# The RWKV part of a decoder layer, from a planner's order to two interleaved streams in a fixed matrix-engine order

## The chip, the cores and the metric

The kernel runs on one core of a Trainium2 chip. The metric is the device time of one launch in microseconds (us), here 2481.27 us as the median of three runs (2479.97 to 2483.46). A core has a matrix engine (PE, with its weight loads PEld), a vector engine (DVE), a scalar engine (ACT), a general engine (POOL) and a queue that issues most DMAs (SP). Each engine runs its own instructions in order; instructions of different engines wait for each other through semaphores.

## The reference, cut to what matters

One decoder layer on 256 tokens with 2048 channels, all in float32. A product with `w_in` feeds three mixers (SSD, RWKV-7, mLSTM) and three gates; each mixer's output is projected, gated and added, then `w_out`, a norm, a convolutional feed-forward block and a norm follow. The change is about RWKV and the gates:

```
proj = h @ w_in
(..., rwkv_p, ..., gate_pre) = split(proj)
merged = (g_ssd * (y_ssd @ proj_ssd) + g_rwkv * (y_rwkv @ proj_rwkv) + g_mlstm * (y_mlstm @ proj_mlstm))

def rwkv7_mixer(p, ...):
    p = p + (token_shift(p) - p) * mu
    r, k, v, w_lo, a_lo, g_lo = split(p)
    decay = exp(-exp(-softplus(-(w0 + tanh(w_lo) @ w2)) - 0.5))
    a = sigmoid(a0 + a_lo @ a2);  g = sigmoid(g_lo) @ g2
    kk = heads(k * k_k);  kk = kk * rsqrt(max(sum(kk * kk), 1e-24))
    kh = heads(k * (1 + (a - 1) * k_a))
    # per step: S = S diag(w) + (S (-kk)) (kk a)^T + v kh^T ;  y = S r
    y = head_layer_norm(recurrence(r, decay, kh, v, -kk, kk * a)) * ln_w + ln_b
    return (y + sum(r * kh * r_k) * v) * g
```

## The kernel before, in words

Weights are float32 and are multiplied in three passes of a reduced float32 type: `chunks` loads two row tiles of 512 columns (512 KB, SP queue, four `wraw` buffers), ACT casts the high half `whi` (L163), and DVE subtracts to get the low half `wlo` (L164); three buffers of each. `proj_cm` then issues 12 products of 128x256 for each row tile (L176, L178, L180), `block_tm` six of 128x512 (L194 to L196, the "wide" ones of the gates). A *chunk* is two row tiles. The loop over chunks is issued at high priority; apart from that, the order of the instructions on every engine is a scheduler's, which simulates the program with a cost for each instruction and picks what is ready.

RWKV's recurrence is done in chunks of 64 tokens, for 4 groups of 8 heads (512 channels). `rwkv_group(g)` first has the products for r, k, v and the gate of branch 1, then the small steps: decays `cs` and `pext`, the norm of k (`nr`, its two halves `nrr`, spread to all rows by L523 and L524, giving `nk` at L525), POOL's `kh` and `av` (L532, L534), and the operands `l1e`/`l1o` (even and odd heads) and `bk`, half on POOL (L552, L554) and half on DVE. Their pair products (L560) go into `bp` with a mask (DVE, L562) and into the other half of l1 (ACT copy L564, POOL mask L565). The diagonal 32x32 blocks of bp are inverted by columns: four DVE transposes (`ni`, L595) bring the matrices into one layout, then 31 steps of two instructions (L610, L612) on the tiles `yi` and `si` run at the same time on DVE (5 columns of the result) and POOL (the other 27). Two transposes to `x1` (L619) and four to `xt` (L622) bring the result back; small products (L630, L639) combine two blocks into one of 64x64. Then four recurrence steps follow (L654 to L688, on `zm`, `zve`, `zvo`), the output gate (L703), and the tail with the head norm and `yo` (L709 to L732).

After the four groups come SSD (two blocks of B and C, then two blocks for each of four groups) and the branches 1, 0, mLSTM and 2. The planner is free to move SSD's weight products up between RWKV's small steps, and does: RWKV and SSD together end at about 897 us. Branch 1 reads its gates from memory (`gdram`), branches 0 and 2 make theirs in `branch` as they go.

`smalls` (its helper lines L403 to L443) prepares the decays of SSD and mLSTM once, by scans on DVE (`s_da`) and small products (L412, L414, L443).

Of the kernel before, what the change touches and what calls it, by code (L numbers as in the profile page):

```python
# [17 lines left out]
P = 128  # L18
# [16 lines left out]
C_R = 5152  # L35
# [20 lines left out]
CONSTS = [("ones", 1), ("head2", 32), ("maskg", 192), ("mneg", 128), ("scanm", 256)]  # L56
# [20 lines left out]
def const_array():  # L77
# [11 lines left out]
    c[:, COFF["scanm"]:COFF["scanm"] + 256] = (np.arange(256) % 64 != 0)[None]  # L89
    c[:, COFF["eps"]:COFF["eps"] + 4] = np.array([1e-5, 64e-5, 1e-6, 1.0], np.float32)[None]  # L90
# [3 lines left out]
class Pair:  # L94
# [8 lines left out]
    def l(self, kt):  # L103
        return self.lo[kt // self.n][:, kt % self.n]


class Layer:
# [61 lines left out]
    def proj_cm(self, W, pieces, cts, X, nkt=KT):  # L169
        nc = self.nc  # L170
        acc = [self.psA.tile([P, 2, T], F32, name="acc") for _ in range((len(cts) + 1) // 2)]
        for kt, wh, wl in self.chunks(W, nkt, pieces):
            for j, (o, m) in enumerate(cts):
# [7 lines left out]
                                 stop=kt == nkt - 1, skip_group_check=True)  # L181
        return [acc[j // 2][:m, j % 2] for j, (o, m) in enumerate(cts)], acc
# [4 lines left out]
    def block_tm(self, W, c0, X, nkt=KT, pages=()):  # L187

# [10 lines left out]
        for kt, wh, wl in self.chunks(W, nkt, [(0, c0, 512)], pages):  # L199
            mm(0, kt, wh, wl)  # L200
            if kt // KC < (nkt + KC - 1) // KC - len(pages):
                mm(1, kt, wh, wl)
            else:
                late.append((kt, wh, wl))
        for w in late:
            mm(1, *w)
# [248 lines left out]
    def rwkv_group(self, g):  # L455
        nc, tc, a = self.nc, self.tc, self.a
        W = a["w_in"]
        vec, gps = nc.vector, nc.gpsimd

        lw = self.lw if g else self.load_lora(0)  # L460

        rkv = []
        for i, (nm, c0, pi) in enumerate((("r", C_R, 0), ("k", C_K, 1), ("v", C_V, 2 + g % 2))):
            cts, _ = self.block_cm(W, c0 + g * 512, self.X)
            t = self.p4(pi, nm)
            for j in range(4):
                self.lerp(cts[j], t[:, j], self.v("mu_" + nm, 4 * g + j),
                          self.omm[:, 16 * i + 4 * g + j:16 * i + 4 * g + j + 1])
            rkv.append(t)
            if g == 0 and i == 0:  # L470
                self.smalls()
        if g == 0:
            for o, i_ in self.spill:
                nc.sync.dma_start(out=o, in_=i_)
        gate = self.gate(1, g, 18)
        nc.scalar.dma_start(out=self.gdram[:, g], in_=gate)
        r, k, v = rkv

# [27 lines left out]

        sq = self.p4(7, "sq")
        for j in range(4):
            nc.scalar.activation(out=sq[:, j], in_=k[:, j], func=AF.Square, scale=self.v("k_k", 4 * g + j))
        ps = self.bank()  # L510
# [7 lines left out]
        self.split(nrr[:, 0], nrr[:, 1], nr)  # L518
        nk = self.p4(8, "nk")
        for ct in range(4):  # L520
# [5 lines left out]
                                     in1=ps, op0=ALU.mult, op1=ALU.mult)  # L526

# [4 lines left out]
        gps.tensor_tensor(out=kh, in0=kh, in1=k, op=ALU.mult)  # L532

        gps.tensor_tensor(out=av, in0=av, in1=nk, op=ALU.mult)  # L534

        sq = self.p4(7, "sq")
        for j in range(4):
            vec.scalar_tensor_tensor(out=sq[:, j], in0=r[:, j], scalar=self.v("r_k", 4 * g + j),
                                     in1=kh[:, j], op0=ALU.mult, op1=ALU.mult)


        L1, BK, BP, ZV = self.L1, self.BK, self.BP, self.ZV
# [4 lines left out]
        PL = self.cp.tile([P, 16], F32, name="pl", bufs=2)  # L547
        vec.tensor_copy(out=PL, in_=pe[:, :, 64])
        for c in range(4):
            for e in range(2):  # L550
# [4 lines left out]
                vec.tensor_tensor(out=uc(BK)[h, c, :, o], in0=ch(kh)[h, c], in1=ch(cs)[h, c], op=ALU.mult)  # L555
            for e in range(2):
                ps = self.bank().rearrange("p (c t) -> p c t", c=4)
                for p in range(4):
                    u = 4 * p + c
                    nc.tensor.matmul(ps[:, p], lhsT=BK[H[e], u], rhs=L1[e][H[e], u], start=True, stop=True)  # L560
                mg = mge[e]
                vec.tensor_tensor(out=uc(BP)[H[e], c], in0=ps[H[e]], in1=mg[H[e]].to_broadcast([64, 4, P]), op=ALU.mult)  # L562
                lk = uc(L1[e])[H[1 - e], c]
                nc.scalar.copy(out=lk, in_=ps[H[1 - e]])  # L564
# [385 lines left out]
    def run(self, upto=None):  # L950
# [7 lines left out]
        for g in range(4):  # L958
            self.rwkv_group(g)
# [144 lines left out]
```

## Time and profile before

| | value |
|---|---|
| median of 3 runs | 2481.27 us |
| the profiled execution | 2480.85 us, of it 2479.1 us of span |
| PE busy in the span | 2397.7 us |
| DVE, ACT, POOL busy | 1681.8, 1250.0, 516.1 us |
| stretch of RWKV and SSD | about 90 to 897 us |
| PE busy in that stretch, granted clock | 762.31 of 807.00 us, 0.96 |
| DVE busy in that stretch | 688.10 us |

The profile's lines name an engine, an operation, the tile written and the tiles read, the shapes and a count; times are us, unless marked ns. The granted clock is the share of full speed that PE had. A line with `<-` behind a bracket names what ended the idle time ahead of the instruction. In a timeline, the first column is the start and the second the length; instructions of one kind that follow closely are merged with their count, and the next one can start before the length shown is over, since matrix products are pipelined. The span is the time between the first and last instruction; the launch's time is a little longer.

### The profile page before, as it was taken

The page shows a single profiled execution, that of the slowest core. Times are in us where ns is not written, and L with a number is a line of the kernel's source. Part 1 is how long each engine was busy: PE and PEld are TensorE (multiplying, and loading weights), DVE is VectorE, ACT ScalarE, POOL GpSimd, SP SyncE. Part 2 cuts the span into 40 slices and gives each one's busy share as a digit, 9 for nine tenths or more (in the row PEclk, how much of TensorE's full clock was granted, in tenths as well). Part 3 has the DMA queues.
Part 4 walks back from the last instruction along what each step waited for, and adds up shares of the span by engine and source line. Part 5 has one row for each costly group of instructions (what it writes and reads, how often), then busy time and mean ns, then how long its engine had stood idle before and what let it go on. Part 6 is the DMA issues. An engine that isn't in the chain of part 4 may idle for free.

```text
span 2479.1 us, 41687 instructions
## 1 busy us (share of the span) xinstructions
PE 2397.7 (97%) x16602; PEld 2164.2 (87%) x16602; DVE 1681.8 (68%) x2116; ACT 1250.0 (50%) x1634; POOL 516.1 (21%) x488
## 2 busy tenths in 40 slices
PE   7999998989999999999999999999999999999997
PEld 7988797887989988888988888887999999998886
DVE  6678988897997875545566665556765666665545
ACT  4555555454646654444456654444554454454333
POOL 0046463563643521001000021000300000000000
PEclk9999998998999999999999999999999999999999
DMA  8654435344445656666666666655655555557664
GB/s 239 187 162 126 134 103 151 86 137 141 121 140 163 193 182 213 211 195 192 184 186 178 181 211 213 188 192 190 186 182 186 181 182 185 186 167 229 195 196 148
DMA packets 280276, 435.09 MB, mean 176 GB/s; under 512 B 25432, under 2 KB 118032, under 8 KB 279696
## 3 DMA queue, kind: packets, MB, share of 16 engines
q1 hardware_dynamic: 278640, 427.70, 56.9%
q8 instruction: 130, 2.13, 0.4%
q10 hardware_dynamic: 864, 2.62, 0.3%
q0 software_dynamic: 576, 2.10, 0.2%
q14 instruction: 66, 0.54, 0.1%
HBM read 423.90 MB, written 8.43 MB: 174 GB/s over the span
## 4 chain that ended last, share of the span: by engine, by line
PE 83%; DVE 10%; issue 2%; POOL 2%; DMA 1%; ACT 1%; SPq 0%; DVEq 0%; POOLq 0%; ACTq 0%
PE acc L195 13%; PE acc L196 13%; PE acc L194 13%; PE acc L180 13%; PE acc L178 13%; PE acc L176 13%; DVE wlo L164 4%; PE mix L560 1%; DVE si L612 1%; DVE si L610 1%; DVE xt L622 1%; DMA wraw<-in_ffn_w_down 1%; DVE ni L595 1%; PE seq L685 1%; PE mix L797 0%
## 5 line engine op out<-in xcount | busy, mean ns | idle before, releaser
L164 DVE TENSOR_TENSOR wlo<-wraw,whi 128x1024 fp32r<-128x1024 f32 (+2 forms) x756 | 987.5, 1309 | 664.6 <-ACT whi L163 656.6
L163 ACT CAST whi<-wraw 128x1024 fp32r<-128x1024 f32 (+2 forms) x756 | 786.9, 1043 | 847.1 <-PE acc L196 427.6
L180 PE MATMUL acc<-xh,wlo 128*128 128x256 f32 x3104 | 889.3, 287 | 21.0 <-DVE wlo L164 20.8
L176 PE MATMUL acc<-xh,whi 128*128 128x256 f32 x3104 | 889.1, 287 | 3.3 <-ACT whi L163 3.1
L178 PE MATMUL acc<-xl,whi 128*128 128x256 f32 x3104 | 887.5, 286 | 0.0
L180 PEld LDWEIGHTS acc<-xh,wlo 128*128 128x128 f32 x3104 | 600.0, 194 | 29.5 <-DVE wlo L164 25.5
L176 PEld LDWEIGHTS acc<-xh,whi 128*128 128x128 f32 x3104 | 601.0, 194 | 9.1 <-ACT whi L163 3.5
L178 PEld LDWEIGHTS acc<-xl,whi 128*128 128x128 f32 x3104 | 601.0, 194 | 3.2 <-issue 1.0
L195 PE MATMUL acc<-wlo,xh 128*128 128x512 f32 x640 | 256.6, 401 | 9.8 <-DVE wlo L164 9.6
L196 PE MATMUL acc<-whi,xl 128*128 128x512 f32 x640 | 252.7, 395 | 0.0
L194 PE MATMUL acc<-whi,xh 128*128 128x512 f32 x640 | 231.8, 394 | 0.0
L195 PEld LDWEIGHTS acc<-wlo,xh 128*128 128x128 f32 x640 | 121.7, 190 | 37.1 <-DVE wlo L164 12.6
L194 PEld LDWEIGHTS acc<-whi,xh 128*128 128x128 f32 x640 | 121.3, 190 | 25.3
L196 PEld LDWEIGHTS acc<-whi,xl 128*128 128x128 f32 x640 | 121.7, 190 | 23.9
L195 PE MATMUL acc<-wlo,ah 128*128 128x512 f32 x322 | 125.5, 390 | 0.5 <-DVE wlo L164 0.5
L196 PE MATMUL acc<-whi,al 128*128 128x512 f32 x322 | 125.3, 389 | 0.0
L1015 POOL TENSOR_TENSOR fc<-fc 128x512 f32<-128x512 f32 (+1 forms) x22 | 28.0, 1271 | 449.2 <-DVE fc L302 444.3
L194 PE MATMUL acc<-whi,ah 128*128 128x512 f32 x322 | 112.1, 389 | 0.4 <-ACT whi L163 0.4
L924 POOL TENSOR_TENSOR merged<-merged,gate 128x512 f32<-128x512 f32 x16 | 28.3, 1787 | 338.5 <-DVE gate L923 338.5
L302 DVE SCALAR_TENSOR_TENSOR fc<-acc,fcols,fc 128x255 f32<-128x255 f32 (+1 forms) x172 | 76.9, 477 | 14.0 <-ACT fc L299 12.5
L275 POOL TENSOR_TENSOR res<-res,gb 128x1024 f32<-128x1024 f32 x16 | 44.3, 2771 | 198.5 <-PE mix L224 88.3
L612 POOL TENSOR_TENSOR yi<-yi,si 128x26 f32<-128x26 f32 (+12 forms) x104 | 73.2, 704 | 7.8
(360 smaller groups left out, 3133.9 us busy)
## 6 DMA issues: line engine op xcount, KB each, us to landing
wraw<-in_w_in SPq DMA_DIRECT2D x368, 512.0 KB, 3.6
wraw<-in_ffn_w_up SPq DMA_DIRECT2D x336, 256.0 KB, 3.1
wraw<-in_ffn_w_down SPq DMA_DIRECT2D x84, 512.0 KB, 4.4
wraw<-in_proj_rwkv SPq DMA_DIRECT2D x32, 512.0 KB, 4.4
wraw<-in_proj_ssd SPq DMA_DIRECT2D x32, 512.0 KB, 3.8
wraw<-in_proj_mlstm SPq DMA_DIRECT2D x32, 512.0 KB, 3.8
wraw<-in_w_out SPq DMA_DIRECT2D x32, 512.0 KB, 4.2
acb<-acd SPq DMA_DIRECT2D x16, 256.0 KB, 3.7
```

The source lines that it names most:

```text
L163: nc.scalar.copy(out=hi[:, :n, :width], in_=r)
L164: nc.vector.tensor_tensor(out=lo[:, :n, :width], in0=r, in1=hi[:, :n, :width].bitcast(F32), op=ALU.subtract)
L176: nc.tensor.matmul(a, lhsT=wh[:, o:o + m], rhs=X.h(kt), start=st, stop=False, skip_group_check=True)
L178: nc.tensor.matmul(a, lhsT=wh[:, o:o + m], rhs=X.l(kt), start=False, stop=False, skip_group_check=True)
L180: nc.tensor.matmul(a, lhsT=wl[:, o:o + m], rhs=X.h(kt), start=False, stop=kt == nkt - 1, skip_group_check=True)
L194: nc.tensor.matmul(acc[tt], lhsT=X.h(kt)[:, s], rhs=wh, start=kt == 0, stop=False)
L195: nc.tensor.matmul(acc[tt], lhsT=X.h(kt)[:, s], rhs=wl, start=False, stop=False)
L196: nc.tensor.matmul(acc[tt], lhsT=X.l(kt)[:, s], rhs=wh, start=False, stop=kt == nkt - 1)
L275: nc.gpsimd.tensor_tensor(out=r[j], in0=r[j], in1=gb[:, i].unsqueeze(1).to_broadcast([P, 2, 512]), op=op)
L302: nc.vector.scalar_tensor_tensor(out=dst[:, j:], in0=ps[:, :T - j], scalar=v(wname, (width - 1 - j) * nch + ct), in1=dst[:, j:], op0=ALU.m ...
L612: eng.tensor_tensor(out=t[:, j + 1:32, lo:e], in0=t[:, j + 1:32, lo:e], in1=tv, op=ALU.subtract)
L924: gps.tensor_tensor(out=m[:, tt], in0=m[:, tt], in1=g[:, tt], op=ALU.add)
```

## The change

`rwkv_group` is cut into generators: `pre` (lora, norm, kh), `pairs`, `inverse`, `recurrence`, `output_gate`, `tail`. They form one stream; the other is the weight products, one row tile at a time: v and gate of group 0, then k, v, r and gate of the next group each, and after these all eight gates of branches 0 and 2. PE's order is no longer the scheduler's: it is the order in which the code issues (`manual_schedule`), and where a generator yields n, n row tiles of the weight stream are issued. The other engines keep the scheduler. In `weave` the yields of the second generator issue nothing. All twelve gates are stored, and `branch` loads them. The first products r and k of group 0 and the `smalls` come before the fixed order. SSD's products follow after RWKV.

After the inverse's first `yield 6` follow yields of 6, 6, 7, 7, 6 and 3 around the products that use v, x1 and xt, and each of the four recurrence steps has three yields of 2.

Inside the steps: the pair products and the small products of L630 take even and odd heads by turns; l1's mask moves to DVE (ACT's copy and POOL's mask go); bk's transposes use another pair of accumulators; the additions for yo move from POOL to DVE. The inverse is new: ACT copies the diagonal blocks together, one transpose of 128 rows makes `ni`, POOL does all 31 steps, on columns that are folded in two halves (62 instructions on 2 x 2856 elements, against 52 on 2 x 3276 before), a DVE shuffle unfolds the result, and one transpose of 128 rows each makes x1 and xt.

```
-        for g in range(4):
-            self.rwkv_group(g)
+        self.rwkv()
+
+    def rwkv(self):
...
+        def groups():
+            yield from self.pre(0)
+            for g in range(4):
+                yield from self.pairs(g)
+                yield from weave(self.inverse(g), self.tail(g - 1) if g else iter(()))
+                yield from weave(self.recurrence(g), self.beside(g))
+            yield from self.tail(3)
+
+        with tc.manual_schedule(engines={mybir.EngineType.PE}):
+            for n in groups():
+                for _ in range(n):
+                    if not next(weights, False):
+                        next(gates, None)
...
+def weave(a, b):
+    for n in a:
+        yield n
+        next(b, None)
+    yield from b
...
+    def beside(self, g):
+        yield from self.output_gate(g)
+        if g < 3:
+            yield from self.pre(g + 1)
...
         self.split(nrr[:, 0], nrr[:, 1], nr)
+        yield 5
         nk = self.p4(8, "nk")
...
+            if ct == 1:
+                yield 1
...
         gps.tensor_tensor(out=av, in0=av, in1=nk, op=ALU.mult)
+        yield 2
...
+        operands(0)
+        yield 4
+        for c in range(4):
+            if c < 3:
+                operands(c + 1)
...
+            for p in range(4):
+                u = 4 * p + c
+                for e in range(2):
+                    nc.tensor.matmul(pss[e][:, p], lhsT=BK[H[e], u], rhs=L1[e][H[e], u], start=True, stop=True)
...
-                nc.scalar.copy(out=lk, in_=ps[H[1 - e]])
-                gps.tensor_tensor(out=lk, in0=lk, in1=mg[H[1 - e]].to_broadcast([64, 4, P]), op=ALU.mult)
+                vec.tensor_tensor(out=uc(L1[e])[H[1 - e], c], in0=ps[H[1 - e]],
+                                  in1=mg[H[1 - e]].to_broadcast([64, 4, P]), op=ALU.mult)
+            yield 2
...
+        for q in range(4):
+            nc.scalar.copy(out=Dg[rows[q]], in_=BP[rows[q], :, 64 * (q // 2) + 32 * (q % 2):][:, :, :32])
+        vec.transpose(out=N.rearrange("p t (h u) -> p t h u", h=2),
+                      in_=Dg.rearrange("p u t -> p t u").unsqueeze(2).to_broadcast([P, 32, 2, 16]))
...
+        for j in range(31):
+            w, e = 31 - j, j // 2 + 1
...
+            gps.tensor_tensor(out=tv, in0=Yo[:, j:j + 1, :e].to_broadcast(sh),
+                              in1=N[:, j + 1:32, j:j + 1].to_broadcast(sh), op=ALU.mult)
+            gps.tensor_tensor(out=Yo[:, j + 1:32, :e], in0=Yo[:, j + 1:32, :e], in1=tv, op=ALU.subtract)
+        vec.stream_shuffle(out=Yc[:, :, :, 1], in_=Yo, mask=[i % 16 + 16 for i in range(32)])
+        vec.transpose(out=X1.rearrange("p u s -> p s u"), in_=Y.rearrange("p t s -> p s t"))
+        vec.transpose(out=XT.rearrange("p u t -> p t u")[:, 0:32], in_=Y)
...
+        yield 6
-        gps.tensor_tensor(out=yo, in0=yo, in1=v, op=ALU.add)
-        gps.tensor_tensor(out=yo, in0=yo, in1=gg, op=ALU.mult)
+        vec.tensor_tensor(out=yo, in0=yo, in1=v, op=ALU.add)
+        vec.tensor_tensor(out=yo, in0=yo, in1=gg, op=ALU.mult)
...
-            if i == 1:
-                g = self.pg("p%d" % (4 + j % 2), [P, 2, 512], "gate")
-                nc.sync.dma_start(out=g, in_=self.gdram[:, j])
-            else:
-                g = self.gate(i, j, 4 + j % 2)
+            g = self.pg("p%d" % (4 + j % 2), [P, 2, 512], "gate")
+            nc.sync.dma_start(out=g, in_=self.gdram[:, i, j])
```

Three places show what moves. The line numbers are each kernel's own. First, PE's order at the start, where the scan's products (L412, L414 before; L438, L440 after) and those of L443 (after: L469) stand among the weight products L176 to L180 (after: L197 to L201). Before:

```order
L176 MATMUL acc<-xh,whi 128x256
L178 MATMUL acc<-xl,whi 128x256
L180 MATMUL acc<-xh,wlo 128x256
L412 MATMUL mix<-cst,s_da 128x32 x4
L414 MATMUL mix<-cst,s_da 128x32
L176 MATMUL acc<-xh,whi 128x256
L178 MATMUL acc<-xl,whi 128x256
```

After:

```order
L199 MATMUL acc<-xl,whi 128x256
L201 MATMUL acc<-xh,wlo 128x256
L438 MATMUL mix<-cst,s_da 128x32 x4
L440 MATMUL mix<-cst,s_da 128x32
L469 MATMUL mix<-cst,s_gs 128x8 x2
L561 MATMUL mix<-wlo__765,lw 128x256 x2
L197 MATMUL acc<-xh,whi 128x256
```

Before, 243 weight products stand ahead of L412 and 19 more between it and s_gs; after, 198 stand ahead, and s_gs follows at once.

Second, PE's order where group 0's first pair products stand, l1e and l1o being the operands of even and odd heads. Before (134 weight products lie between the last L524 and this):

```order
L180 MATMUL acc<-xh,wlo 128x256
L176 MATMUL acc<-xh,whi 128x256
L560 MATMUL mix<-l1e,bk 128x128 x4
L560 MATMUL mix<-l1o,bk 128x128 x4
L178 MATMUL acc<-xl,whi 128x256
L180 MATMUL acc<-xh,wlo 128x256
```

After (36 products and 30 wide ones lie between the last L608, which was L524, and this):

```order
L220 MATMUL acc<-wlo,xh 128x512
L221 MATMUL acc<-whi,xl 128x512
L671 MATMUL mix<-l1e,bk 128x128
L671 MATMUL mix<-l1o,bk 128x128
L671 MATMUL mix<-l1e,bk 128x128
L671 MATMUL mix<-l1o,bk 128x128
L671 MATMUL mix<-l1e,bk 128x128
L671 MATMUL mix<-l1o,bk 128x128
L671 MATMUL mix<-l1e,bk 128x128
L671 MATMUL mix<-l1o,bk 128x128
```

The halves now go by turns, and less work lies ahead of them. POOL's queue keeps its order there: av, eight l1, then eight bk.

Third, DVE's order at the end of group 0's inverse. Before:

```order
L610 TENSOR_TENSOR si<-si,ni 128x5
L612 TENSOR_TENSOR si<-si 128x5
L613 COPY yi<-si 128x32x5
L164 TENSOR_TENSOR wlo<-wraw,whi 128x1024
L619 STREAM_TRANSPOSE x_1860<-yi 32x32x32 x2
L622 STREAM_TRANSPOSE xt<-yi 32x32x32 x4
L164 TENSOR_TENSOR wlo<-wraw,whi 128x1024 x3
```

After:

```order
L181 TENSOR_TENSOR wlo<-wraw,whi 128x1024
L320 SCALAR_TENSOR_TENSOR k<-acc,cst,k 128x255
L181 TENSOR_TENSOR wlo<-wraw,whi 128x1024 x2
L714 STREAM_SHUFFLE yi<-yi 128x512
L716 STREAM_TRANSPOSE x_1848<-yi 128x32x32
L718 STREAM_TRANSPOSE xt<-yi 128x32x32
L181 TENSOR_TENSOR wlo<-wraw,whi 128x1024 x4
```

DVE's own steps are gone; between the transpose to ni and the shuffle, which needs POOL's last step, ten wlo stand in group 0 and nine or ten in the others, and the rest stand behind. In groups 1 and 3 one wlo stands between the shuffle and the transposes.

More of the change, by code (lines that the diff above doesn't have):

```diff
@@ L104, in l, with whole @@
         return self.lo[kt // self.n][:, kt % self.n]
+def whole(units):
+    while True:
+        try:
+            next(units)
+        except StopIteration as e:
+            return e.value
+def weave(a, b):
[3 more added lines that the diff above has]
+    yield from b
 class Layer:
@@ L204, in block_tm @@
                 late.append((kt, wh, wl))
+            yield True
         for w in late:
@@ new lines, in rkv_units @@
+    def rkv_units(self, g, nm, page, after):
+        c0 = {"r": C_R, "k": C_K, "v": C_V}[nm]
+        cts, _ = yield from self.cm_units(self.a["w_in"], [(0, c0 + g * 512, 512)],
+                                          [(P * j, P) for j in range(4)], self.X)
+        while after is not None and after not in self.done:
+            yield False
+        t = self.p4(page, nm)
+        i = "rkv".index(nm)
+        for j in range(4):
+            self.lerp(cts[j], t[:, j], self.v("mu_" + nm, 4 * g + j),
+                      self.omm[:, 16 * i + 4 * g + j:16 * i + 4 * g + j + 1])
+        self.t[nm, g] = t
@@ new lines, in rwkv @@
+    def rwkv(self):
+        nc, tc = self.nc, self.tc
+        self.t, self.done = {}, set()
+        lw = self.load_lora(0)
+        whole(self.rkv_units(0, "r", 0, None))
+        self.smalls()
+        whole(self.rkv_units(0, "k", 1, None))
+        for o, i_ in self.spill:
+            nc.sync.dma_start(out=o, in_=i_)
+        weights, gates = self.weights_of_groups(), self.weights_of_gates()
+        self.lw = lw
+        def groups():
[10 more added lines that the diff above has]
+                        next(gates, None)
+            for rest in (weights, gates):
+                for _ in rest:
+                    pass
@@ L505, in rwkv_group @@
             self.lw = self.load_lora(g + 1)
+        while ("k", g) not in self.t:
+            yield 1
+        k = self.t["k", g]
         sq = self.p4(7, "sq")
@@ L546, in rwkv_group, with operands @@
         pec, mge = uc(pe), [self.c("maskg", 64 * e, P).unsqueeze(1) for e in range(2)]
-        PL = self.cp.tile([P, 16], F32, name="pl", bufs=2)
-        vec.tensor_copy(out=PL, in_=pe[:, :, 64])
-        for c in range(4):
+        def operands(c):
             for e in range(2):
@@ L613, in rwkv_group @@
[L613 to L624 removed]
+        yield 6
```

224 lines of the change are left out of this document (132 added, 92 removed).

## The prediction

> **What bounds the kernel now.** I read four views in this order: the page's busy times, a table of two stretches of the span, the waits in the first, and timelines around the waits that the change touches. First the page and the stretches (busy time of PE, PEld, DVE, ACT and POOL, then granted clock, DMA share, GB/s).
>
> ```profile
> PE 2397.7 (97%) x16602; PEld 2164.2 (87%) x16602; DVE 1681.8 (68%) x2116; ACT 1250.0 (50%) x1634; POOL 516.1 (21%) x488
> 90.00:897.00 807.00, 762.31 (x6705) 698.96 (x6704) 688.10 (x950) 442.65 (x659) 391.25 (x408) 0.96 0.49 143
> 897.00:2479.00 1582.00, 1562.75 (x9309) 1393.21 (x9307) 933.73 (x1075) 758.74 (x911) 123.07 (x72) 1.00 0.61 190
> 800.00:900.00 100.00, 97.41 (x803) 93.06 (x802) 85.16 (x109) 62.63 (x83) 45.68 (x24) 1.00 0.64 190
> ```
>
> The matrix engine bounds the whole. The stretch from 90 to 897 us is RWKV and SSD, and only it has much to gain: PE idles 807.00 − 762.31 = 45 us there, and a granted clock of 0.96 costs another 0.04 × 807 = 32 us. After 897 us PE is short of work for 19 us in 1582. So 77 us is the most that a better order of the same products could win. The waits of that stretch (total us, times, longest) and the price of a clock that has dropped:
>
> ```profile
> PE acc L180 <- DVE wlo L164: 19.5, 18, 3.6
> ...
> 173.81 0.28 PE L180 MATMUL acc<-xh,wlo 128*128 128x256 f32 x1
> 173.93 0.28 PE L176 MATMUL acc<-xh,whi 128*128 128x256 f32 x1
> 176.19 1.14 PE L560 MATMUL mix<-l1e,bk 64*128 64x128 f32 x5 [1.98 <-POOL bk L554]
> ...
> 176.00:178.00 2.00, 1.81 (x12) 1.81 (x13) 1.55 (x2) 1.74 (x3) 1.85 (x3) 0.63 0.00 0
> 178.00:180.00 2.00, 2.00 (x9) 1.78 (x9) 2.00 (x3) 0.00 (x0) 1.93 (x2) 0.50 0.00 0
> 180.00:182.00 2.00, 2.00 (x11) 2.00 (x11) 1.36 (x3) 1.27 (x2) 1.77 (x4) 0.50 0.56 132
> 182.00:184.00 2.00, 2.00 (x13) 2.00 (x13) 1.38 (x1) 0.93 (x2) 1.93 (x2) 0.66 0.34 130
> ```
>
> The largest single cause is DVE: it is busy 85% of the stretch and brings the low halves of the weights late. The matmuls of 256 columns start 0.12 us apart (173.81, 173.93); a chunk, which is 24 of them, lasts 2.88 us. One wait of 1.98 us before the first pair product is followed by clocks of 0.63, 0.50, 0.50 and 0.66: (0.37 + 0.50 + 0.50 + 0.34) × 2 us = 3.4 us lost behind the wait. I charge that to each long wait.
>
> **The terms of the change.** *Products laid side by side.* Pairs now alternate between l1e and l1o, which use different row halves.
>
> ```profile
> 186.20 1.16 PE L560 MATMUL mix<-l1e,bk 64*128 64x128 f32 x8
> ...
> 323.72 0.27 PE L560 MATMUL mix<-l1e,bk 64*128 64x128 f32 x1
> 323.74 0.27 PE L560 MATMUL mix<-l1o,bk 64*128 64x128 f32 x1
> 323.83 0.27 PE L560 MATMUL mix<-l1e,bk 64*128 64x128 f32 x1
> ...
> 263.15 1.19 PE L630 MATMUL seq<-x,bp 32*32 32x32 f32 x32 [0.42 <-DVE x L619]
> ```
>
> Where both halves happened to alternate, two matmuls start 0.02 us apart and the next of the first half 0.11 us on (323.72, 323.74, 323.83); eight of one half take 1.16 us, (1.16 − 0.27) / 7 = 0.13 from one start to the next. So a pair costs what a single one did, and 128 of the 256 pair products vanish beside others: 128 × 0.11 = 14 us. The 256 products of L630 take 1.19 / 32 = 0.037 us each; half of them beside others saves 128 × 0.037 = 5 us. Together −19 us, on PE itself.
>
> *Less DVE work.* These groups shrink or leave DVE (busy us, mean ns):
>
> ```profile
> L164 DVE TENSOR_TENSOR wlo<-wraw,whi 128x1024 fp32r<-128x1024 f32 x191 | 274.0, 1441 | 66.7 <-ACT whi L163 65.9
> ...
> L610 DVE TENSOR_TENSOR si<-si,ni 128x60 f32<-128x60 f32 (+29 forms) x124 | 51.6, 416 | 2.6
> L612 DVE TENSOR_TENSOR si<-si 128x60 f32<-128x60 f32 (+29 forms) x124 | 49.2, 397 | 2.6
> ...
> L595 DVE STREAM_TRANSPOSE ni<-bp 32x1024 f32<-32x1024 f32 x16 | 32.3, 2019 | 0.3
> L622 DVE STREAM_TRANSPOSE xt<-yi 32x1024 f32<-32x1024 f32 x16 | 31.1, 1946 | 0.4
> L619 DVE STREAM_TRANSPOSE x<-yi 32x1024 f32<-32x1024 f32 x8 | 16.9, 2110 | 0.4
> L562 DVE TENSOR_TENSOR bp<-mix,cst 64x512 f32<-64x512 f32 x32 | 22.0, 687 | 13.3 <-PE mix L560 12.7
> ```
>
> The DVE inverse (101 us) goes, 40 transposes of 32 rows (80 us) become 12 of 128 rows (24 us if such a row also costs 2.0 us), 32 masks are added (22 us) and 8 yo additions (10 us, by 1.2 for an instruction of 128x1024). That is about −125 us of 688, which removes the throughput reason for late weights. It makes no time by itself: it can only take away the 45 us of idle. A 128-row transpose is not in the trace; between 2.0 us and 8 us (four quarters in turn, 4 × 2.0) I take 2.0, because its rows have the same 1024 elements.
>
> *Masks before the pairs' end, transposes in another buffer set, yo additions on DVE:* the yo additions and masks are in DVE's queue behind weights and cost nothing while DVE has its 125 us to spare; without it, 22 + 10 us. The copies that ACT loses and gains (masked halves, diagonal blocks) lie on an engine busy for 443 of 807 us and cost nothing but the one copy in the chain of D.
>
> *The 8 gate blocks of branches 0 and 2* move from the branch stage, where PE is full, to the RWKV stage: the same PE work at either place, 0. What the SSD blocks hid before lies bare instead: the SSD stage alone showed 2.6 us idle in 100 (row 800 to 900), and about 250 us of it now stands by itself: S = +6 us. The gates' stores go to ACT's queue and their loads to SP's; those loads stand among weight loads that run four buffers ahead, so I cost them nothing. Uncovered, each of the 8 would be a load from issue to landing; the nearest row (KB each, median us) gives 8 × 3.7 = 30 us:
>
> ```profile
> acb<-acd SPq DMA_DIRECT2D x16, 256.0 KB, 3.7
> ```
>
> *The start, once (E).* s_da is scanned on DVE and PE uses it at once:
>
> ```profile
> 96.69 0.74 DVE L403 TENSOR_TENSOR_SCAN s_da<-cst,s_adt 32x128 f32<-32x128 f32 x2
> 97.45 1.07 PE L412 MATMUL mix<-cst,s_da 32*128 32x32 f32 x8
> 101.20 0.61 PE L443 MATMUL mix<-cst,s_gs 8*128 8x8 f32 x4
> 103.96 0.61 PE L443 MATMUL mix<-cst,s_em 8*128 8x8 f32 x4
> ```
>
> L412 already starts 0.02 us after the scan's end. In the new order the same product (L438) stands 45 weight matmuls earlier, 5.4 us; s_gs follows without the 19 matmuls (2.3 us) that lay before it; em has 12 instead of 17. E = +8 us.
>
> *The norm to the first pair (A, C).* Group 0 of before, from the norm to the first pair product at 176.19:
>
> ```profile
> 150.27 0.41 DVE L212 TENSOR_TENSOR nrr<-nr,nrr 128x256 fp32r<-128x256 f32 x1
> 157.68 0.27 PE L524 MATMUL mix<-nrr,ones 32*128 32x256 f32 x1
> 161.57 0.87 DVE L525 SCALAR_TENSOR_TENSOR nk<-k,cst,mix 128x256 f32<-128x256 f32 x2
> 162.53 3.33 POOL L534 TENSOR_TENSOR av<-av,nk 128x1024 f32<-128x1024 f32 x1 [4.11 <-DVE nk L525]
> 165.81 1.72 POOL L552 TENSOR_TENSOR l1e<-nk,pext 64x256 f32<-64x256 f32 x1
> 173.13 0.64 POOL L552 TENSOR_TENSOR l1o<-nk,pext 64x256 f32<-64x256 f32 x1
> 175.42 8.94 POOL L554 TENSOR_TENSOR bk<-av,cs 64x256 f32<-64x256 f32 x8
> ```
>
> Before, 134 weight matmuls stood between L524 and the first pair: 157.68 to 176.19 is 18.5 us, and 1.98 us of it was a wait. POOL alone takes 176.19 − 162.53 = 13.7 us: av, eight l1, the first bk. The new order fixes the cover: 36 matmuls and 30 wide ones in group 0, 60 matmuls in groups 1 and 2, 30 wide ones in group 3. A wide one has twice the columns, so at most 0.24 us: 11.5, 7.2, 7.2 and 7.2 us, 33.1 in all. POOL's queue still has all eight l1 ahead of the first bk, and DVE's has other work ahead of the last two nk. The whole chain from the end of nrr (150.68) is 25.5 us; with the first four l1 at 0.7 us like the last four, rather than 1.6, it is 21.9. Its cover, with the 12 matmuls between the L608s, is 33.1 + 4 × 1.4 = 38.7. So C lies between 4 × 21.9 − 38.7 = 49 and 4 × 25.5 − 38.7 = 63; if nk follows its product at once, POOL's part alone against the cover gives 4 × 13.7 − 33.1 = 22. I take 50: the last four l1 of the row ran at 0.64 and DVE has less to do, while the late nk stay. A is the wait from k's squares to nrr in groups 1 to 3. That chain has six small instructions like nrr and nk (0.41 and 0.44 us) and their handovers, an estimated 5 us, against 12 wide matmuls, 2.9 us: 2 us each, A = 6 (3 to 15).
>
> *The inverse (D).* It leaves DVE for POOL, and behind its end stands a shuffle in DVE's queue, ahead of the weights' low halves. From group 0 of before:
>
> ```profile
> 213.85 0.25 POOL L610 TENSOR_TENSOR si<-yi,ni 128x26 f32<-128x26 f32 x1 [2.05 <-DVE ni L595]
> 214.18 1.30 POOL L612 TENSOR_TENSOR yi<-yi,si 128x26 f32<-128x26 f32 x1
> ...
> 213.90:252.40 38.50, 20.75 (x45) 34.48 (x52) 1.00 0.48 138
> 213.90:252.40 38.50, 22.54 (x71) 13.38 (x71) 13.33 (x11) 1.00 0.48 138
> ```
>
> The first window row is for the inverse's temporary (DVE, POOL), the second for wlo (PE, PEld, DVE). POOL needed 38.5 us for 52 instructions on 2 × 3276 elements, while DVE ran 11 wlo and its own 45. The same size takes 0.25 or 1.30 us, so a DVE instruction beside it costs POOL about 1.05 us. Now 62 instructions on 2 × 2856 elements: unblocked 34.48 − 11 × 1.05 = 22.9, scaled by their number to 27; with the 10 or so wlo that stand beside them, 27 + 10 = 37. I take 35, the upper end less what DVE's shorter masks leave free.
>
> The Trainium skill, "SBUF — State Buffer", section on the two separate sides, calls the port pair that the two engines share an exclusive lock: a DVE instruction with two SBUF inputs blocks a POOL instruction that reads SBUF for its whole length. The two lengths of the same size agree with it. By that rule alone the 34 us of DVE in the two rows would be most of POOL's 34.48, and the new inverse would take 62 × 0.25 + 10 × 1.25 = 28 us: D about 10 and a sum of 2501, on the way to the first rival.
>
> From the last pair: masks 4 × 0.69, a copy, a wlo of 1.3 and the transpose of 2.0 make 6.7; the inverse 35; shuffle 0.7 (a DVE instruction of that size); X1 and XT 4.0 and the next wlo 1.3: 47.7 us. PE's feed ahead of the shuffle is 13 chunks in group 0, 12 in the others: 13 × 2.88 + 3.6 of small products = 41, then 37.5, 37.5 and 35.3. Where one wlo stands between shuffle and transposes PE takes it at 43.7 and then runs dry again. The waits are 7, 9, 11 and 13: D = 40, between 8 (inverse 27) and 65 (inverse at the 41 us that 34.48 × 62 / 52 gives).
>
> *The recurrence* has weights by turns after each step, and one wlo between zm and its use: F = 5 (0 to 15).
>
> **The sum.** Idle of after: 8 + 6 + 50 + 40 + 5 + 6 = 115, before 45: +70. Clock: nine long waits × 3.4 = 31, before 32: −1. Side by side −19. So 2480.85, the profiled execution's own time, + 70 − 1 − 19 = 2531; that execution lies 0.4 us below the median, which changes nothing.
>
> **Rivals.** (1) *The other side: POOL runs free.* While DVE stands at the shuffle, and has lost its own inverse, nothing blocks POOL. Then the inverse takes 27 and D is 8; l1 at 0.64 takes 5 us off each C, 30; five long waits cost 17 us of clock. Idle 63, +18; −15; −19: 2465. It decides where the inverse on POOL is under about 31 us. For it: the 0.25 us instruction. Against: 10 wlo stand in the same stretch. With C at its bound of 22 and no A, F or E it would reach 2440.
> (2) *Nothing seen*, idle 63 to 80 with the same clock: 2476 to 2486.
> (3) *Transposes in quarters:* 8 us each puts 18 us more on each D: 2531 + 72 less what C hides, about 2590.
>
> **How the numbers follow.** 0.2% is 5 us, about what a measurement of this kernel can tell from no change. Chances: waits as summed, 2500 to 2575, 0.60; POOL free, 2440 to 2475, 0.25; no change 0.06; quarters 0.06; beyond, 0.03. The range from 2440 to 2580 leaves under 2 in 10 out; the likeliest case alone has 2500 to 2575. Faster 0.26, same 0.06, slower 0.68.
>
> **What would show it.** Right: PE waiting 10 us or more before the first pair product in each group for POOL's bk; a DVE wait at the shuffle for POOL, and PE waiting for wlo behind it; pair products 0.11 us for two. Wrong: POOL's l1 ahead of pairs by more than the cover, an inverse under 31 us, nk right behind its product, or the DVE rows of 128 partitions far from 2.0 us.

## The result: 2.2% slower, 2534.85 us, and the profile after

| | before | after |
|---|---|---|
| median of 4 runs | 2480.93 us | 2534.85 us (2532.81 to 2538.96) |
| ratio after to before, 95% interval | | 1.0218 (1.0200 to 1.0235) |
| profiled execution | 2480.85 us | 2534.50 us |

The page's busy times of after, and two stretches of it (columns as before; RWKV and SSD now end at about 930 us, the gates of branches 0 and 2 included):

```profile
PE 2386.7 (94%) x16602; PEld 2145.2 (85%) x16602; DVE 1541.7 (61%) x1884; ACT 1252.6 (49%) x1629; POOL 437.2 (17%) x484
90.00:930.00 840.00, 734.03 (x5918) 639.81 (x5917) 485.10 (x590) 414.60 (x594) 258.55 (x380) 0.93 0.48 141
930.00:2532.00 1602.00, 1579.99 (x10097) 1433.38 (x10096) 996.61 (x1203) 789.48 (x971) 177.79 (x98) 0.99 0.61 191
```

Every engine but ACT has less to do, and it takes longer. PE is busy 11 us less and DVE 140 us less; DVE is at 58% of the first stretch instead of 85%. But PE idles 840.00 − 734.03 = 106 us there, against 45, at a clock of 0.93. Its waits, over the whole trace (total us, times, longest):

```profile
PE acc L220 <- DVE wlo L181: 27.9, 11, 6.2
PE mix L671 <- POOL bk L656: 23.7, 5, 8.8
PE acc L201 <- DVE wlo L181: 19.1, 8, 9.5
...
PE seq L866 <- ACT yo L870: 7.5, 8, 1.4
PE acc L219 <- DVE r L320: 6.1, 2, 3.1
PE mix L438 <- DVE s_da L429: 5.1, 1, 5.1
```

The two places that the prediction named stand out: the first pairs (bk) and wlo. In group 1, the wait ahead of the pairs, first on PE, then on POOL, then on DVE:

```profile
318.62 0.28 PE L201 MATMUL acc<-xh,wlo 128*128 128x256 f32 x1
326.66 0.80 PE L671 MATMUL mix<-l1e,bk 64*128 64x128 f32 x2 [7.76 <-POOL bk L656]
...
313.94 2.37 POOL L621 TENSOR_TENSOR av<-av,nk 128x1024 f32<-128x1024 f32 x1 [7.22 <-DVE nk L609]
316.26 1.71 POOL L654 TENSOR_TENSOR l1e<-nk,pext 64x256 f32<-64x256 f32 x1
325.09 0.72 POOL L654 TENSOR_TENSOR l1o<-nk,pext 64x256 f32<-64x256 f32 x1
325.89 4.79 POOL L656 TENSOR_TENSOR bk<-av,cs 64x256 f32<-64x256 f32 x5
...
309.51 3.44 DVE L657 TENSOR_TENSOR bk<-kh,cs 64x256 f32<-64x256 f32 x8
312.99 0.87 DVE L609 SCALAR_TENSOR_TENSOR nk<-k,cst,mix 128x256 f32<-128x256 f32 x2
314.91 5.81 DVE L181 TENSOR_TENSOR wlo<-wraw,whi 128x1024 fp32r<-128x1024 f32 x3
```

Read from below: the last two nk stand behind eight bk on DVE, so POOL starts av at 313.94; eight l1 follow before the first bk, and PE, which ran out of products at 318.9, goes on at 326.66. The three wlo behind nk show the side effect: PE had already waited 2.5 us for one of them, until 317.44. In group 0, the end of the inverse:

```profile
217.43 0.28 PE L199 MATMUL acc<-xl,whi 128*128 128x256 f32 x1
227.24 0.58 PE L201 MATMUL acc<-xh,wlo 128*128 128x256 f32 x1 [9.53 <-DVE wlo L181]
...
209.83 1.23 DVE L181 TENSOR_TENSOR wlo<-wraw,whi 128x1024 fp32r<-128x1024 f32 x1 [1.38 <-ACT whi L180]
221.04 1.28 DVE L714 STREAM_SHUFFLE yi<-yi 128x512 f32<-128x512 f32 x1
222.36 2.02 DVE L716 STREAM_TRANSPOSE x<-yi 128x1024 f32<-128x1024 f32 x1
224.22 1.91 DVE L718 STREAM_TRANSPOSE xt<-yi 128x1024 f32<-128x1024 f32 x1
225.94 2.37 DVE L181 TENSOR_TENSOR wlo<-wraw,whi 128x1024 fp32r<-128x1024 f32 x2
...
183.40:221.10 37.70, 32.70 (x62) 1.00 0.50 149
183.40:221.10 37.70, 26.03 (x92) 17.64 (x92) 12.81 (x10) 1.00 0.50 149
```

The wlo that PE needs at 217.7 is started at 225.94, behind the shuffle, which waits for POOL until 221.04; DVE does nothing from 211 on. The last two rows are the stretch of the inverse, for its temporary on POOL and for wlo (PE, PEld, DVE): 62 instructions in 37.7 us, beside ten wlo.

Over the whole trace I added up all distances between two PE starts above 0.7 us, less one product's own spacing: 56.9 us before, 128.4 after, +71. Time at half clock outside these costs half of itself: 30.5 and 42.9, +12. The rest, the work itself with its small gaps, falls by 30. The sum, +53, is the difference of the spans (2532.7 − 2479.1 = 53.6). These three parts, waits, half clock and work, are used again below.

### The profile page after: what moved, and what is told of

Read it like the earlier page. It is cut to its first block, busy times and chain, and to the rows that moved or that the text cites. A ratio compares the mean times of both kernels' runs of the same rounds, so it can differ in the third digit from the quotient of the medians.

```text
span 2532.7 us, 41457 instructions
## 1 busy us (share of the span) xinstructions
PE 2386.7 (94%) x16602; PEld 2145.2 (85%) x16602; DVE 1541.7 (61%) x1884; ACT 1252.6 (49%) x1629; POOL 437.2 (17%) x484
## 4 chain that ended last, share of the span: by engine, by line
PE 79%; POOL 8%; DVE 5%; DMA 3%; issue 3%; ACT 2%; SPq 0%; DVEq 0%; ACTq 0%; POOLq 0%
PE acc L197 13%; PE acc L201 13%; PE acc L199 13%; PE acc L219 11%; PE acc L220 11%; PE acc L221 11%; POOL si L711 3%; POOL yi L713 3%; DVE wlo L181 2%; ACT whi L180 1%; PE mix L671 1%; POOL l1o L654 1%; POOL l1e L654 1%; DMA wraw<-in_w_in 1%; PE mix L561 1%
## 5 line engine op out<-in xcount | busy, mean ns | idle before, releaser
L181 DVE TENSOR_TENSOR wlo<-wraw,whi 128x1024 fp32r<-128x1024 f32 (+2 forms) x756 | 974.4, 1291 | 781.6 <-ACT whi L180 773.0
L180 ACT CAST whi<-wraw 128x1024 fp32r<-128x1024 f32 (+2 forms) x756 | 787.2, 1043 | 920.9 <-PE acc L221 424.9
L201 PE MATMUL acc<-xh,wlo 128*128 128x256 f32 x3104 | 883.9, 285 | 19.1 <-DVE wlo L181 19.1
L197 PE MATMUL acc<-xh,whi 128*128 128x256 f32 x3104 | 889.8, 287 | 10.2 <-ACT whi L180 5.0
L201 PEld LDWEIGHTS acc<-xh,wlo 128*128 128x128 f32 x3104 | 599.6, 193 | 22.0 <-DVE wlo L181 20.7
L197 PEld LDWEIGHTS acc<-xh,whi 128*128 128x128 f32 x3104 | 600.0, 193 | 17.3 <-ACT whi L180 5.6
L219 PE MATMUL acc<-whi,xh 128*128 128x512 f32 x640 | 256.2, 413 | 8.1 <-DVE r L320 6.1
L711 POOL TENSOR_TENSOR si<-yi,ni 128x126 f32<-128x126 f32 (+22 forms) x124 | 64.9, 523 | 121.4 <-DVE ni L698 84.7
L220 PEld LDWEIGHTS acc<-wlo,ah 128*128 128x128 f32 x322 | 60.4, 188 | 13.7 <-DVE wlo L181 1.2
```

What stands on the lines that cost most here:

```text
L180: nc.scalar.copy(out=hi[:, :n, :width], in_=r)
L181: nc.vector.tensor_tensor(out=lo[:, :n, :width], in0=r, in1=hi[:, :n, :width].bitcast(F32), op=ALU.subtract)
L197: nc.tensor.matmul(a, lhsT=wh[:, o:o + m], rhs=X.h(kt), start=st, stop=False, skip_group_check=True)
L201: nc.tensor.matmul(a, lhsT=wl[:, o:o + m], rhs=X.h(kt), start=False, stop=kt == nkt - 1, skip_group_check=True)
L219: nc.tensor.matmul(acc[tt], lhsT=X.h(kt)[:, s], rhs=wh, start=kt == 0, stop=False)
L220: nc.tensor.matmul(acc[tt], lhsT=X.h(kt)[:, s], rhs=wl, start=False, stop=False)
```

## The experiments

Each run has its median, the ratio to the kernel before as measured beside it, and the 95% interval of that ratio.

My theory: the fixed order gives the two long chains of each group (norm to pairs, inverse to shuffle) too little cover, that is, too few products that PE can issue meanwhile because they need nothing from the chain, while the planner sized it by their length. The rival: the parts cost the time, whatever the order (the long POOL inverse, gates away from where DVE has room, SSD alone).

**The order alone.** The whole change with the planner's order on PE:

```
-        with tc.manual_schedule(engines={mybir.EngineType.PE}):
+        with nullcontext():
```

> The whole change, but PE's order is left to the planner again (all else stays: new inverse, products by turns, gates moved, generators). Theory: the loss of about 54 us comes from the fixed order giving the long chains too little cover (waits for POOL's bk ahead of the pairs about 25 us, for wlo ahead of them and behind the shuffle about 43, clock 12). The planner puts 15 to 17 us of products between the norm and the pairs instead of 7 to 11, and ten wlo ahead of each shuffle; so the pair waits go, the shuffle waits stay: 2534.85 - 40 - 10 = about 2485, between 2465 and 2500. Rival: the parts themselves cost the time (the long POOL inverse, the gates moved away from where DVE has room, SSD left alone), whatever the order: then it stays above 2515.

2486.34 us, 1.0016 (1.0007 to 1.0026) of before: 48 of the 54 us go with the order. The bk waits at the first pairs fall to 7.6 us; those behind the inverse stay, partly as waits for the inverse itself:

```profile
PE seq L748 <- DVE x L716: 16.2, 2, 9.6
PE acc L220 <- DVE wlo L181: 13.5, 6, 7.0
PE acc L201 <- DVE wlo L181: 12.1, 6, 6.4
PE mix L671 <- POOL bk L656: 7.6, 4, 3.3
```

The rival fails for the loss. But it is right about one thing: with 129 us less on DVE (1552.5 against 1681.8 busy) the other parts together do not gain anything either. By the three parts of the count, the planner's order has 50 us less of waits and 16 less of half clock than the fixed one, and 19 us more of work. One reason for the last is that the planner also orders the pair products: in 9 of its 16 blocks of pairs eight products of each half stand together again, and only 55 of the 256 are followed by one of the other half, against 232 under the fixed order and 32 before. So this run says little of products by turns.

**The inverse's end.** A small PE transpose that stands 17 row tiles behind the start of the inverse, and a one-column copy that reads it, hold the shuffle back in the planner's view (the shuffle, the transposes and the copies behind them move down to that place):

```
-        yield 7
+        yield 4
+        ps = self.bank("seq")
+        nc.tensor.transpose(out=ps[:, :P], in_=v[:, 0, :P], identity=self.c("ident"))
+        vec.tensor_copy(out=Yf[:, 1:2], in_=ps[:, :1])
+        vec.stream_shuffle(out=Yc[:, :, :, 1], in_=Yo, ...)
...
+        yield 3
         yield 6
```

> The change with the shuffle, the two transposes behind it and a one-column copy ahead of it tied to a small PE transpose that stands 17 row tiles behind the start of the inverse, so that the planner places 12 wlo ahead of the shuffle in each group, not 10 and 9; one PE transpose more for each group. Theory: the waits for wlo behind the shuffle (9.7, 5.2, 6.3 and 6.7 us) shrink by the two or three chunks more that PE has, 5.8 or 8.6 us, to about 4 in group 0 and nothing elsewhere: -23 and some 5 of clock, 2505 to 2512. Rival: PE waits there for the inverse itself and only its place changes: the wait moves to the products of x1, and the time stays within 5 us of 2535.

2508.90 us, 1.0105 (1.0084 to 1.0126): −26 against after, in the middle of what was expected. The waits for wlo fall from 47 to 22 us and the bk waits stay:

```profile
PE mix L671 <- POOL bk L656: 24.2, 5, 9.1
PE acc L201 <- DVE wlo L181: 11.1, 8, 2.2
PE acc L220 <- DVE wlo L181: 10.6, 3, 4.2
```

So the wait was DVE's queue, not the inverse as such: in group 0 of after, PE goes on at 227.24 and reaches the first product of x1 at 241.9, so 15 us of products that needed only wlo had stood still.

**POOL's order.** Code order for POOL too, so each bk follows its l1:

```
-        with tc.manual_schedule(engines={mybir.EngineType.PE}):
+        with tc.manual_schedule(engines={mybir.EngineType.PE, mybir.EngineType.Pool}):
```

> The change with POOL's order fixed to the code's as well, so that each bk stands right behind its l1 and the first two bk behind two l1, not eight. Theory: six l1 at 0.7 us or more go from the chain to the first pair, 4.5 to 5 us in each group; the waits for bk of 2.7, 7.9, 8.9 and 5.2 us fall to about 0, 3, 4 and 0, with a little of the clock: 2535 - 17 - 4 = about 2514. Rival: the chain ends not with bk but with DVE's late nk and the wlo behind them, so that the wait moves to wlo: 2525 or more.

2508.14 us, 1.0107 (1.0092 to 1.0122): −27, more than the 21 expected. The bk waits go from 23.7 to 3.3 us and the wlo waits hardly change:

```profile
PE acc L220 <- DVE wlo L181: 27.3, 9, 6.2
PE acc L201 <- DVE wlo L181: 16.8, 6, 9.5
...
PE mix L671 <- POOL bk L656: 3.3, 2, 2.5
```

**Both.** The two edits together.

> The fixed POOL order and the later shuffle together. Theory: they shorten two different waits of each group, so the gains add: 2508.9 - 21 = about 2488. Rival: cover is one stock, and what the pairs no longer wait for the shuffle waits for again, since PE reaches it earlier but POOL's inverse does not start earlier: 2500 to 2509.

2489.11 us, 1.0029 (1.0017 to 1.0040): −46, against −26 and −27 alone. They add up but for 7 us; the rival of one stock (2500 to 2509) is out for these two, because neither takes products from anywhere. In this trace the waits for bk are 8.0 us, not 3.3, and a wait for DVE's k has 6.6 us, where it had 2.6 in after.

**More cover for the pairs.** 8 row tiles moved ahead of them, from behind the inverse:

```
         operands(0)
-        yield 4
+        yield 12
...
-        yield 6
-        yield 7
-        yield 7
-        yield 6
+        yield 4
+        yield 5
+        yield 5
+        yield 4
```

> The change with 8 row tiles (9.6 to 11 us) moved in each group: ahead of the first pair product, taken from behind the inverse; the number of products stays. Theory: the four waits for bk (2.7, 7.9, 8.9, 5.2 us) and the wlo waits just ahead of them (3.8, 2.6, 3.2, 5.4) are covered, with the slow clock behind them: -40 - 8; but the products of x1 then stand 41 us behind the last pair and the chain to them takes 47, so the shuffle's waits stay as they are: 2485 to 2500. Rival: DVE's work between the norm and the pairs (about 8 us without a wlo) makes the waits, not the cover; then the bk waits go and the wlo waits stay: 2505 to 2515.

2524.00 us, 1.0169 (1.0147 to 1.0191): −11, below both forecasts. The bk waits vanish, and as much comes back behind the inverse:

```profile
PE acc L219 <- ACT gate L1050: 23.6, 2, 12.1
PE acc L220 <- DVE wlo L181: 18.9, 5, 11.0
PE acc L201 <- DVE wlo L181: 18.8, 5, 9.2
```

The 23.6 us are two waits for an accumulator at the inverses of groups 1 and 2 (388 and 578 us in that trace), 12 us each where wlo cost 5 and 6. The shuffle is behind them too. The gate empties the accumulator on ACT, and ACT, whose next v stands ahead of it, waits for DVE's v, which stands behind the shuffle; the copies of xt come only after the gate. Group 1, ACT first, then DVE (group 2 shows the same, 11.25 us for v at 587.78):

```profile
397.80 0.47 ACT L319 ACTIVATE v<-acc,omm 128x256 f32<-128x256 f32 x1 [10.62 <-DVE v L320]
399.58 0.60 ACT L1050 ACTIVATE gate<-acc 128x512 f32<-128x512 f32 x1
401.64 0.62 ACT L720 COPY xt<-xt 32x512 f32<-32x512 f32 x1
...
395.05 0.01 DVE L714 LOAD_MASK_SELECT yi<-yi  x1 [9.91 <-POOL yi L713]
395.05 1.28 DVE L714 STREAM_SHUFFLE yi<-yi 128x512 f32<-128x512 f32 x1
397.30 0.47 DVE L320 SCALAR_TENSOR_TENSOR v<-acc,cst,v 128x255 f32<-128x255 f32 x1
```

**Cover from the recurrence.** On top of both edits, 4 row tiles of each group go from the recurrence to the pairs, and the row tile between the nk products goes behind them:

```
-            if ct == 1:
-                yield 1
...
-        yield 2
+        yield 3
...
         operands(0)
-        yield 4
+        yield 8
...
             for e in range(2):
                 nc.scalar.copy(out=ZV[e][H[e], :, c], in_=RU[H[e], 1])
-            yield 2
+            yield 1
```

> As the fixed POOL order with the later shuffle, and 4 row tiles of each group moved from the recurrence (its middle yield 2 to 1) ahead of the first pair, and the four nk products side by side (the row tile between them goes behind). Theory: the pair waits and the wlo waits ahead of them go entirely (another 10 to 15 us), and the recurrence, whose waits are under 1 us each, pays 0.7 us for each of 16 steps: between 2470 and 2485. Rival: the recurrence's chain needs all of its cover, and the time is that of the kernel without this step or more: 2488 to 2500.

2503.57 us, 1.0088 (1.0073 to 1.0103): 14 us slower than without, a miss beyond the rival. The bk waits are gone, wlo waits rise from 24 to 34 us, and a new one appears, PE at L607 for DVE's nk (5.2 us in 4). Two moves stand in one kernel here, the row tiles of the recurrence and the one between the nk products; which of them costs what stays open.

**One part on the old kernel.** Products by turns in the code of the kernel before, for the pairs and in the same way for L630, all else as it was:

```
-            for e in range(2):
-                ps = self.bank().rearrange("p (c t) -> p c t", c=4)
-                for p in range(4):
-                    u = 4 * p + c
-                    nc.tensor.matmul(ps[:, p], lhsT=BK[H[e], u], rhs=L1[e][H[e], u], start=True, stop=True)
+            pss = [self.bank().rearrange("p (c t) -> p c t", c=4) for _ in range(2)]
+            for p in range(4):
+                u = 4 * p + c
+                for e in range(2):
+                    nc.tensor.matmul(pss[e][:, p], lhsT=BK[H[e], u], rhs=L1[e][H[e], u], start=True, stop=True)
...
```

> The kernel before, with one part of the change alone: the pair products and the products of L630 take even and odd heads by turns. Theory: PE is the bound and each product that runs beside another saves its own time, 14 + 5 us: 2480.93 - 19 = about 2462, between 2458 and 2470. Rival: what PE saves there it loses in waits for the low halves of the weights, since DVE is busy for 85% of that stretch: then 2474 to 2483.

2481.02 us, 0.9994 (0.9985 to 1.0004): no gain, against the theory's 19 us. PE is busy 11 us less (2386.8 against 2397.7) and waits 16 us more for wlo; before, these waits were 19.5 us at L180 (shown in the prediction) and, at L195:

```profile
PE acc L195 <- DVE wlo L164: 9.6, 7, 3.3
```

With products by turns:

```profile
PE acc L180 <- DVE wlo L164: 30.4, 19, 7.5
PE acc L195 <- DVE wlo L164: 15.0, 7, 6.3
...
176.97 0.93 PE L560 MATMUL mix<-l1e,bk 64*128 64x128 f32 x6 [2.00 <-POOL bk L554]
185.75 1.16 PE L560 MATMUL mix<-l1e,bk 64*128 64x128 f32 x8
...
90.00:890.00 800.00, 744.52 (x6661) 684.36 (x6660) 686.08 (x943) 442.32 (x657) 397.30 (x408) 0.96 0.49 143
```

The two rows of L560 show that the edit did less than its code says: the planner, which orders PE here, puts most of the products of one half together again. Only 105 of the 256 pair products are followed by one of the other half (32 before). By starts at full clock the pairs take 27.6 us, where they took 32.5 before and 18.5 in after. By the count above PE's own work fell by 9 us, not 19, and 10 us more of waits in all took that back, as the rival said. That DVE, 686 us busy of 800, set the pace there is a reading, not shown by this run.

**Wide transposes on the old kernel.** To test that, ni, x1 and xt by one transpose of 128 rows each, as in the change, with the inverse still split between DVE and POOL:

```
+        Dg = self.pg("p6", [P, 2, 16, 32], "dg")
+        bpv = BP.rearrange("p u (h t) -> p h u t", h=2)
         for q in range(4):
-            vec.transpose(out=N[rows]..., in_=bpv[rows, 32 * b:32 * b + 32])
+            nc.scalar.copy(out=Dg[rows[q]], in_=bpv[rows[q], :, :, 32 * b:32 * b + 32])
+        vec.transpose(out=N, in_=Dg.rearrange("p h u t -> p t (h u)"))
...
-        for q in (0, 2):
-            vec.transpose(out=X1[rows[q]]..., in_=Y[rows[q]]...)
-        for q in (1, 3, 0, 2):
-            vec.transpose(out=xtv[rows[q], 32 * b:32 * b + 32], in_=Y[rows[q]])
+        vec.transpose(out=X1.rearrange("p u s -> p s u"), in_=Y.rearrange("p t s -> p s t"))
+        vec.transpose(out=XT.rearrange("p u t -> p t u")[:, 0:32], in_=Y)
+        for q in (1, 3):
...
+            nc.scalar.copy(out=XT[rows[q], us, 32:64], in_=XT[rows[q], us, 0:32])
...
```

With products by turns as well:

> The kernel before with two parts of the change: products by turns, and one transpose of 128 rows for ni, X1 and XT each instead of four, two and four of 32 rows (four ACT copies ahead, two behind). The inverse stays split between DVE and POOL, the order stays the planner's, gates and masks stay. Theory: products by turns alone gained nothing because DVE was late with wlo; this takes 80 - 25 = 55 us off DVE and some 10 us off the chain behind each inverse, so the 19 us of PE show and some of the 57 us of waits go: 2450 to 2467. Rival: the long wlo waits come from bursts of other DVE work in the same places, not from DVE's sum: 2472 to 2482.

**2448.63 us, 0.9865 (0.9850 to 0.9879): faster than both kernels**, and 1 us below the range of the theory. The granted clock of the stretch rises to 0.99 and the wlo waits halve against those of products by turns alone:

```profile
90.00:890.00 800.00, 767.47 (x6878) 703.30 (x6877) 643.90 (x945) 478.90 (x703) 397.02 (x414) 0.99 0.48 150
PE acc L180 <- DVE wlo L164: 15.8, 15, 3.1
PE acc L195 <- DVE wlo L164: 6.4, 8, 1.7
```

By the count above, the 34 us are 16 of half clock, 10 of waits and 8 of work. The planner undoes the turns in part here too: 96 of the 256 pair products are followed by one of the other half.

Without products by turns:

> The kernel before with the transposes of 128 rows alone, products not by turns. With both, 34 us were gained; with products by turns alone, about 1. Theory: the two are not additive, since DVE was the limit of the stretch: the transposes alone give their 14 to 24 us of shorter waits, and products by turns give the rest only where DVE keeps up: 2458 to 2470. Rival: the transposes carry it all and turns are worth nothing in either kernel: 2446 to 2453.

2461.38 us, 0.9916 (0.9901 to 0.9930). By the same count the 21 us are 13 of waits and 9 of half clock, and no work. So the edit for products by turns, as far as the planner let it stand, is worth 1 us on the old kernel and 13 us on the one with wide transposes; the parts are not additive. That kernel has 56 us less to do on DVE (1625.6 us busy, 1681.8 before), but also a shorter chain behind the inverse; which of the two makes the difference no run separates. Products that truly go by turns were not run on the old kernel.

**The masks.** l1's mask on DVE, as in the change, added to the fastest kernel:

```
-                lk = uc(L1[e])[H[1 - e], c]
-                nc.scalar.copy(out=lk, in_=ps[H[1 - e]])
-                gps.tensor_tensor(out=lk, in0=lk, in1=mg[H[1 - e]].to_broadcast([64, 4, P]), op=ALU.mult)
+                vec.tensor_tensor(out=uc(L1[e])[H[1 - e], c], in0=ps[H[1 - e]],
+                                  in1=mg[H[1 - e]].to_broadcast([64, 4, P]), op=ALU.mult)
```

> The kernel with products by turns and transposes of 128 rows, and l1's mask on DVE, as in the change, in place of an ACT copy and a POOL instruction. DVE gets 32 instructions of 0.69 us, 22 us; POOL loses 39. Theory: wlo is still what PE waits for in that kernel (23 us in long waits), so more DVE work costs a part of its 22 us: 2452 to 2462. Rival: POOL's inverse and the pairs' chain, rid of POOL's masks, come earlier and DVE's slack takes the masks: 2438 to 2447.

2450.03 us, 0.9876 (0.9860 to 0.9893): its interval and that of the kernel without overlap, so it says neither; 20 us more on DVE (1637.9 busy, 1618.1 without) cost nothing that can be told, with 47 us less on POOL. That speaks against DVE's sum alone as the limit.

## Why the prediction was right, and where its terms were off

The two waits that the prediction named came at the places and for the causes that it gave, and its two large rivals are out. But the sum gave 2531 and the chip 2534.85 partly because errors of opposite sign met: C and D were both too large, other waits and the clock too small. That they cancel to 4 us is luck.

- *Idle, +70 forecast, +71 by the count above.* By the prediction's own measure, stretch less busy time, it went from 45 to 106 us, +61. C was forecast at 50. Measured by the distances between starts are 24.8 us at the pairs (2.7, 7.9, 8.9, 5.2) and 15.0 just ahead of them for wlo (3.8, 2.6, 3.2, 5.4): 40. So the sign that the prediction named, 10 us or more for bk in each group, came in none; with the wlo the four are 6.5, 10.5, 12.1 and 10.6. The chain itself was right: from nrr to the first pair 24.2, 23.9, 26.2 and 22.1 us, against 21.9 to 25.5. The cover was mis-sized: I counted 12 matmuls, 1.4 us, between the L608s of every group, but in groups 1 to 3 16 products of the recurrence's end stand there as well (with 12 wide ones in groups 1 and 3), and from the end of nrr to the last L608 pass 3.9, 6.0, 6.8 and 4.5 us. And I did not see that the wait would fall partly on wlo.
- *D, 40 forecast, 28 measured* (9.7, 5.2, 6.3, 6.7). POOL's inverse takes 36.4 to 37.6 us (35 forecast, 27 in the rival), the shuffle 1.28 us (0.7), the transposes of 128 rows 2.0 us as taken; the rival of POOL running free and that of quarters are both out. What was mis-sized is PE's feed: from the last pair to its running dry were 41.2, 40.9, 43.8 and 39.9 us, where I had 41, 37.5, 37.5 and 35.3 (by my own terms 12 × 2.88 + 3.6 = 38.2, not 37.5; about 1 us of D). In groups 1 to 3 the tail of the group before runs in that stretch, whose transposes wait for ACT's yo, two waits in each (0.7 and 1.5 us).
- *E, 8 forecast*: 5.3 us at L438 and 0.8 at s_gs. In the whole traces 621 weight products stand ahead of L412 and 576 ahead of L438, not 243 and 198; the difference of 45, on which E rests, is right. *A, 6 forecast*: 4.9 at L607 and L608.
- *Not forecast*: about 7.5 us for yo, 6.1 for accumulators that DVE's r had not yet freed, 4 for ACT's gate, 2.7 for k. These took the place of what C and D lacked, where I had put 11 for the recurrence and SSD (F and S).
- *Clock, −1 forecast, +12.* There were more half-clock stretches than the nine waits I counted: the trace of after has 16 of them between 90 and 900 us, before has 10.
- *PE's own work, −19 forecast, −30.* The 19 are right: L671 takes 18.5 us where L560 took 32.5, L748 4.5 where L630 took 8.9, by the distances between starts at full clock. They came with the fixed order, which keeps the turns; under the planner's order the same code gave 9 on the old kernel (27.6 and 5.2). The other 12 lie in the small gaps between the 128x256 weight products, 1139.6 us of starts before and 1127.0 after. What shrinks them stays open: with 56 us less on DVE they stay at 1141.4 (wide transposes alone), and the whole change in the planner's order has 1130.6.
- *DVE's work, −125 forecast, −140 measured.* 13 of the other 15 us are in wlo itself: 987.5 us for 756 before, 974.4 after.
- *Rival 2* was added up wrongly: idle of 63 to 80 us at the same clock gives 2480.85 + 18 or 35 − 19, 2480 to 2497, not 2476 to 2486. The time fell outside of both.

The step "it makes no time by itself: it can only take away the 45 us of idle", on the 125 us less of DVE, was too narrow. In the kernel before, 56 us off DVE, which also shortens the chain behind the inverse, gave 21 us by themselves, and 9 of them through the clock (0.97 against 0.96), which that step left out.

The sentence on the Trainium skill, "SBUF — State Buffer", section on the two separate sides, gave an inverse of 28 us and a sum of 2501. The rule agrees with the rows at the end of this document; my use of it was wrong, because it took 0.25 us for every instruction and no time between them. The 10 long ones take 13.17 us together, so the other 52 average (32.70 − 13.17) / 52 = 0.38 us, and the gaps make 37.70 − 32.70 = 5.0 us.

## What to carry to other kernels

A fixed order turns each chain's cover into a number that someone has to count: write down the chain's length from the trace and the products behind which it hides, place by place, and look at every queue that the chain passes, since a wait on DVE or POOL holds up what stands behind it there. Moving cover from one chain to another that is short as well gained little here (11 us); taking work out of the chain and putting the blocked work ahead of the blocker gained 27 and 26, and 46 of the 54 together. Count in the trace whether an edit to the code's order has reached the engine: a scheduler that orders the engine can undo it, as it did with more than half of the turns. And take the cheap parts of a large change one by one on the old kernel: here two of them gave −34 us, where the whole gave +54.

## What the runs showed of the hardware

A stream transpose of 128 rows by 1024 elements takes as long as one of 32 rows: 2.09 against 2.02 us (ni after and before). A stream shuffle of 128x512 takes 1.28 us, about twice a product of 64x512 with a mask (0.69). At full clock, two pair products of one half start 0.126 us apart, two of different halves 0.061 on average (193 such steps before, 231 after). Beside DVE, POOL's steps of one size take 1.35 or 0.39 us. Group 0's inverse has 10 long ones among 62, and ten wlo run in it. One of them, DVE first, then POOL:

```profile
187.03 1.23 DVE L181 TENSOR_TENSOR wlo<-wraw,whi 128x1024 fp32r<-128x1024 f32 x1 [2.58 <-ACT whi L180]
192.76 1.27 DVE L738 TENSOR_TENSOR v<-v,mix 128x512 f32<-128x512 f32 x2
...
187.18 1.35 POOL L711 TENSOR_TENSOR si<-yi,ni 128x81 f32<-128x81 f32 x1
188.60 0.39 POOL L713 TENSOR_TENSOR yi<-yi,si 128x81 f32<-128x81 f32 x1
193.18 0.40 POOL L713 TENSOR_TENSOR yi<-yi,si 128x96 f32<-128x96 f32 x1
```

The instruction that starts during wlo ends just behind it (188.53 and 188.26). The two of L738, with one input from an accumulator, leave POOL's step at 193.18 at its short length.
